# A ninth pair of gate/up tiles by seven products, with differences and low parts on GpSimd and a second norm that starts its x2 early

## The chip, the cores and the metric

The kernel runs on one NeuronCore of a Trainium2 chip. The core has a matrix engine (TensorE, PE), two engines for elementwise work with different strengths (VectorE, DVE; ScalarE, ACT), a general one (GpSimd, POOL) and a queue processor for transfers (SyncE, SP); PE writes to PSUM, all others work from SBUF or PSUM. The metric is the device time of one execution in microseconds. The median of several runs counts, and one more execution is recorded by the hardware profiler.

## The reference

One inference step of one layer, for a prompt of 1024 rows and a sample of 64 rows, all in fp32:

```python
def _layer(x, c, ...):
    mod = (silu(c) @ w_ada + b_ada)             # six shifts, scales and gates
    u = rmsnorm(x, g_pre_mix) * (1 + sc_m) + sh_m
    q, k, v, xr, yr, ga, gr = split(u @ w_in)
    attn_o = windowed_attention(q, k, v)        # 16 heads, 4 kv heads, window 128
    xc = causal_conv(xr);  h = rglru(xc)        # gated linear recurrence, 1280 wide
    rnn_o = h * gelu(yr)
    merged = sigmoid(ga) * (attn_o @ w_attn_o) + sigmoid(gr) * (rnn_o @ w_rnn_o)
    x = x + gt_m * rmsnorm(merged @ w_out, g_post_mix)
    u = rmsnorm(x, g_pre_ffn) * (1 + sc_f) + sh_f
    f = (silu(u @ w_ffn_gate) * (u @ w_ffn_up)) @ w_ffn_down
    return x + gt_f * rmsnorm(f, g_post_ffn)
```

The model width is 1024, the feed-forward width 2816, that is 22 tiles of 128 (`NF`). The new keys, values, convolution rows and states are returned too.

## The kernel before

Activations lie transposed, channels on the partitions and the 1088 rows (1024 + 64) along the free axis. A product in fp32 precision is made of three faster ones in the format fp32r: each operand is split into a high part (a copy rounded to fp32r) and a low part (what the rounding left), and `dense` adds high by high, high by low and low by high in PSUM. The high part of a weight (`wh`) is a copy on ACT, line 159, the low part (`wl`) a difference on DVE, line 163. `Stream` loads the weights over SP, keeps four raw tiles (`RAW`) and up to six split ones (`LIVE`) ahead.

The order of every engine's instructions is fixed when the kernel is built. `Sched` keeps a clock for each engine from estimated costs (`S.t`); PE's clock is `S.now`. Side work is written as generators in a heap: `dense` and the pair products give them a turn after each matmul (`S.poll`), and a generator that has yielded a time comes on when PE's clock has passed it. So the costs in `Sched`, not the chip, decide where in PE's row a transpose or a norm's product stands. The chip then runs each engine's row in this order and waits where an input isn't there.

The stages, by the trace: projections and norm from the start to about 72 us, then q and recurrent projections with attention beside them to 433 us, further projections and the recurrence to 759 us, the attention's and the recurrence's output projections to 977 us, the projection `w_out` with norms to 1084 us, gate and up tiles to 1573 us, the product with `w_ffn_down` to about 1848 us, and the last norm.

*Attention.* `attention()` (line 1097) goes through eight pairs of heads with nine `unit(j, t)` each (line 970), eight row tiles and the sample. A unit makes scores on PE (tag `sc`), then a softmax on DVE and ACT; after that four transposes (line 141, tag `pt`, from `s`) and a copy to `pts` on ACT. The products with V (tag `po`) of a unit are held back in `att["pv"]` and made by `run_pv` ahead of the next unit's transposes. Scores, transposes and these products lie between the matmuls of the projections (tag `d`). `attention()` waits at the end of each pair until all nine units are done.

*Norm chains.* `fin_chain(c)` (line 1429) follows the projection `w_out` for chunk c of 364, 364 and 360 columns. It makes a first norm from squares and products with ones (tag `ms` or `po`, `norm_stats`, line 544), takes the root (`rstd_of`), broadcasts by a product with `sel` (tag `pt`), forms x2 = x + gated norm in place of `mix`, m = 0 to 7, by two or three DVE instructions each, sends it to DRAM (`d_x2`) and takes the second norm's squares as each x2 tile is made; then come root and broadcast again and `make_u`, which writes u2 as high and low part (`u2h`, `u2l`). For the third chunk the squares of the second norm are added up on DVE into one tile first (`fold`, in `nb`), so that PE has one set of products with ones to do.

*Gate and up.* `NPLAIN` = 6 of the 22 tiles are made plainly by `f_tile` (line 1533), for each chunk 24 + 24 matmuls, then silu on ACT, the product on DVE (line 163, `hst<-hst,ps_d`), the high part on ACT, the low part on DVE (`hst<-hst`) and a store to `d_h` on POOL's queue. The order of tiles and chunks is `plain_jobs`: tiles 0 to 3 are spread so that the first two chunks are worked on while the third chunk's norm chain runs, tiles 4 and 5 come last. The other 16 tiles are made as eight pairs by `gu_pair` and `pair_product`: a 2 x 2 block product by seven instead of eight multiplications, with 168 matmuls of 272 columns for gate and as many for up. The right-hand factors are made once by `right_factors` (line 1557): per tile two sums `rec` of high and low part, four differences `tf` of 272 columns, their high part `rh` (ACT) and low part `rl` (DVE). All of this except `rh` is on DVE; the helper `calm` holds it until DVE's clock is less than 0.3 us ahead of PE's. The left-hand factors are sums of weight tiles `s1` to `s4` on DVE in `Stream.source`.

## Time and profile before

| | us |
|---|---|
| median of 3 runs (lowest, highest) | 1865.53 (1863.71, 1867.55) |
| the profiled execution's own time | 1862.13 |
| its span on the core | 1860.4 |
| PE busy | 1829.2 (98%), 12532 instructions |
| DVE busy | 1128.8 (61%), 2405 |
| ACT busy | 887.5 (48%), 1844 |
| POOL busy | 225.5 (12%), 371 |
| granted clock of TensorE, mean | 0.997 of full |

PE is busy when a matmul runs; its weight loads run beside it in a row of their own. The span is the time on the core from the first to the last recorded instruction, the own time of the execution is a little longer. A busy share is a mean over all stages, so stretches are read apart in the rows below. A group of instructions is named by line, engine, operation, output and inputs; behind the bar stand its busy time, the mean of one in ns, and the engine's idle time just ahead of them with what ended it.

### The profile page before, as it was taken

What the parts mean: (1) busy time and instruction counts of PE and PEld (TensorE: products, weight loads), DVE (VectorE), ACT (ScalarE), POOL (GpSimd) and SP (SyncE); (2) the same over time, 40 slices, a digit from 0 to 9 for tenths busy, and PEclk for the clock granted to TensorE, in tenths of its full rate; (3) what the DMA queues carried; (4) which work ended last, traced back from release to release, by engine and by line L of the source; (5) the groups of instructions that cost most, each with busy time, mean ns of one, the idle gap of its engine ahead of it and who ended that gap; (6) DMA issues with size and microseconds to landing.
All of it is one profiled execution on the core that took longest, in us unless ns stands there. A gap on an engine that the chain in (4) does not pass through costs nothing.

```text
span 1860.4 us, 32480 instructions
## 1 busy us (share of the span) xinstructions
PE 1829.2 (98%) x12532; PEld 1771.7 (95%) x12532; DVE 1128.8 (61%) x2405; ACT 887.5 (48%) x1844; POOL 225.5 (12%) x371
## 2 busy tenths in 40 slices
PE   7999999999999999999999999999999999999997
PEld 4999999999999999999999999999999999999997
DVE  6755556555877865264676878755556555245354
ACT  6655556654776665211225555433433344243444
POOL 0011111111111000201001111000000003212021
PEclk9999999999999999999999999999999999999998
DMA  8122212124344344955445554422222236959474
GB/s 330 58 67 76 83 60 71 66 97 151 117 150 174 112 151 152 396 166 210 141 152 180 181 177 153 141 71 99 98 94 94 96 109 233 349 175 337 125 227 126
DMA packets 116170, 281.15 MB, mean 151 GB/s; under 512 B 14800, under 2 KB 24272, under 8 KB 116016
## 3 DMA queue, kind: packets, MB, share of 16 engines
q1 hardware_dynamic: 81216, 155.71, 25.7%
q0 software_dynamic: 34800, 123.38, 18.4%
q8 instruction: 98, 1.61, 0.4%
q14 instruction: 56, 0.46, 0.1%
HBM read 210.46 MB, written 68.57 MB: 150 GB/s over the span
## 4 chain that ended last, share of the span: by engine, by line
PE 85%; issue 6%; DMA 4%; DVE 2%; ACT 2%; POOL 1%; SPq 0%; POOLq 0%; ACTq 0%; DVEq 0%
PE ps_d L132 67%; PE ps_sc L132 11%; PE ps_po L132 3%; PE ps_pt L141 2%; PE ps_pt L132 2%; DMA ho<-d_h 2%; DMA wr<-w 1%; DMA d_h<-hl 1%; ACT kh L159 1%; DMA xre<-d_x 1%; PE ps_ms L132 1%; ACT wh L159 1%; DMA x<-xT 0%; DVE wl L163 0%; POOL ho L186 0%
## 5 line engine op out<-in xcount | busy, mean ns | idle before, releaser
L163 DVE TENSOR_TENSOR wl<-wr,wh 128x512 fp32r<-128x512 f32 (+2 forms) x424 | 277.4, 674 | 232.4 <-ACT wh L159 231.5
L159 ACT ACTIVATE wh<-wr 128x512 fp32r<-128x512 f32 (+2 forms) x424 | 253.0, 610 | 269.3 <-PE ps_d L132 158.5
L132 PE MATMUL ps_d<-uh,wl 128*128 128x364 f32 (+1 forms) x1080 | 357.4, 331 | 0.0
L132 PE MATMUL ps_d<-uh,wh 128*128 128x364 f32 (+1 forms) x1080 | 356.4, 330 | 0.1
L132 PE MATMUL ps_d<-ul,wh 128*128 128x364 f32 (+1 forms) x1080 | 355.8, 329 | 0.6 <-DVE ul L167 0.6
L132 PE MATMUL ps_d<-ho,wh 128*128 128x416 f32 (+1 forms) x924 | 221.4, 327 | 3.6 <-ACT wh L159 2.5
L132 PEld LDWEIGHTS ps_d<-ul,wh 128*128 128x128 f32 x1080 | 203.1, 188 | 3.8 <-DVE ul L167 1.8
L132 PEld LDWEIGHTS ps_d<-uh,wl 128*128 128x128 f32 x1080 | 203.1, 188 | 2.3 <-issue 1.7
L132 PEld LDWEIGHTS ps_d<-uh,wh 128*128 128x128 f32 x1080 | 202.9, 188 | 1.7 <-ACT uh L159 1.4
L132 PEld LDWEIGHTS ps_d<-ho,wh 128*128 128x128 f32 x924 | 162.6, 190 | 6.1 <-ACT wh L159 2.9
L132 PE MATMUL ps_d<-ho,wl 128*128 128x416 f32 (+1 forms) x462 | 150.8, 326 | 0.7 <-DVE wl L163 0.7
L132 PE MATMUL ps_d<-u2h,wl 128*128 128x364 f32 (+2 forms) x480 | 150.6, 314 | 0.0
L132 PE MATMUL ps_d<-u2l,wh 128*128 128x364 f32 (+2 forms) x480 | 149.9, 312 | 0.0
L132 PE MATMUL ps_d<-u2h,wh 128*128 128x364 f32 (+2 forms) x480 | 149.8, 312 | 0.0
L159 ACT ACTIVATE wh<-ws 128x512 fp32r<-128x512 f32 x64 | 40.1, 627 | 112.5 <-DVE ws L163 112.5
L132 PEld LDWEIGHTS ps_d<-u2h,wl 128*128 128x128 f32 x480 | 90.2, 188 | 0.4
L132 PEld LDWEIGHTS ps_d<-u2h,wh 128*128 128x128 f32 x480 | 90.3, 188 | 0.0
L132 PEld LDWEIGHTS ps_d<-u2l,wh 128*128 128x128 f32 x480 | 90.3, 188 | 0.0
L132 PEld LDWEIGHTS ps_d<-ho,wl 128*128 128x128 f32 x462 | 87.7, 190 | 1.7 <-DVE wl L163 1.1
L167 DVE SCALAR_TENSOR_TENSOR adac<-ada,cs,adac 128x512 f32<-128x512 f32 x112 | 78.2, 745 | 14.4 <-DMA ada<-w_ada 14.4
L163 DVE TENSOR_TENSOR wl<-ws,wh 128x512 fp32r<-128x512 f32 x64 | 44.3, 692 | 67.9 <-ACT wh L159 67.1
L159 ACT ACTIVATE pts<-ps_pt 128x512 f32<-128x512 f32 (+2 forms) x80 | 40.0, 511 | 83.0 <-PE ps_pt L141 80.4
(350 smaller groups left out, 4325.5 us busy)
## 6 DMA issues: line engine op xcount, KB each, us to landing
wr<-w SPq DMA_DIRECT2D x268, 256.0 KB, 3.2
wr<-w_dn SPq DMA_DIRECT2D x120, 256.0 KB, 3.5
ho<-d_h POOLq DMA_DIRECT2D x44, 416.0 KB, 9.1
ada<-w_ada SPq DMA_DIRECT2D x48, 256.0 KB, 3.0
gl<-d_ga POOLq DMA_DIRECT2D x16, 544.0 KB, 6.7
d_h<-hh POOLq DMA_DIRECT2D x16, 544.0 KB, 4.2
d_h<-hl POOLq DMA_DIRECT2D x16, 544.0 KB, 5.4
ada<-w_ada SPq DMA_DIRECT2D x16, 512.0 KB, 9.7
```

Source lines behind the costliest of these rows:

```text
L132: self.nc.tensor.matmul(out, lhsT=w, rhs=x, start=start, stop=stop, skip_group_check=part)
L141: self.nc.tensor.transpose(out, in_, ident)
L159: self.nc.scalar.activation(out, in_, func, bias=bias, scale=scale, **kw)
L163: self.nc.vector.tensor_tensor(out, a, b, op=op)
L167: self.nc.vector.scalar_tensor_tensor(out, in0=a, scalar=s, in1=b, op0=op0, op1=op1)
```

## The change

1. `NPLAIN` goes from 6 to 4: tiles 4 and 5 leave the plain stage and become a ninth pair.
2. The factors' signs are chosen so that every difference is one subtraction: `s2` to `s4`, `t1` to `t4`, `partial`, `total`, and the last steps of gate and up no longer need a factor of -1.
3. A new helper `S.pool` issues an elementwise instruction on GpSimd. The four differences `tf` of each tile go there, and so does the low part of a plain tile's h, in a generator `finish` of its own; its store stays on POOL's queue behind it. `right_factors` makes up to two tiles at a time, each with its own `rec` and `tf`, and waits until six slots are free (five before); DVE's clock may be `CALM` = 1.5 us ahead.
4. `fin_chain` makes x2 in a generator `x2_make` that runs ahead of the squares by `AHEAD`; `norm_stats` issues the add of a folded square one step later.
5. A unit's transposes, with the held products with V ahead of them, become a generator `transposed` in a list `post`. The next unit takes them on right behind its scores, or the unit itself after 2.6 us. `attention()` goes to the next pair of heads when the nine units' scores are issued, and frees the pair's q then.

The core of the diff:

```diff
-NPLAIN = 6
+NPLAIN = 4
+CALM = 1.5
+AHEAD = 1.0
...
+    def pool(self, out, a, b, op, after=0.0):
+        self.nc.gpsimd.tensor_tensor(out, a, b, op=op)
+        return self._fin("pool", self._n(out) * 3.1e-3 + 0.05, after)
...
             if kind == "s2":
-                return s2, S.tt(s2, s1, a11, OP.add), 0
+                return s2, S.tt(s2, s1, a11, OP.subtract), 0
...
             f = S.act(sq, src, AF.Square, after=t)
+            if held:
+                add_up()
             if 0 < k < fold:
-                f = S.tt(ring[0][:, 0:n], ring[0][:, 0:n], sq, OP.add, after=f)
-                sq = ring[0][:, 0:n]
+                held.append((sq, f))
             if k >= fold - 1:
+                if held:
+                    sq, f = add_up()
                 pend.append((k, sq, f))
...
+        for g in post[:1]:
+            advance(g)
         t_sc = S.now + 0.1
...
+        g = [transposed(), S.now]
+        post.append(g)
+        limit = S.now + 2.6
+        while S.now < limit and g in post:
+            yield S.now + 0.1
+        while g in post:
+            advance(g)
+            yield max(g[1], S.now + 0.02)
...
-            dones = []
-            yield S.now + 1.0
             head_setup(j)
...
-            while not all(d[0] for d in dones):
-                yield S.now + 0.2
+            while att["sc"] < 9 * (j + 1):
+                yield S.now + 0.1
...
-        def x2_src():
+        done = []
+
+        def x2_make():
             for m in range(8):
...
-                yield mx(m), f
+                done.append((mx(m), f))
+                yield f - AHEAD
+
+        S.spawn(x2_make())
...
+    def finish(st, hi, lo, f2, dst, n):
+        yield f2 - 0.3
+        f3 = S.act(hi, lo, AF.Copy, after=f2)
+        yield f3 - 0.3
+        f4 = S.pool(lo, lo, f32(hi), OP.subtract, after=f3)
+        S.dma(QP, dst, f32(st[:, 0:2, 0:n]), after=f4)
+        st.free()
...
-            S.tt(t1, b11, b12, OP.subtract)
-            S.stt(t2, t1, -1.0, b22, OP.mult, OP.subtract)
-            S.tt(t3, b22, b12, OP.subtract)
-            f = S.stt(t4, t2, -1.0, b21, OP.mult, OP.subtract)
+            yield f - 0.3
+            for o, a, b in ((t1, b12, b11), (t2, b22, t1), (t3, b22, b12), (t4, b21, t2)):
+                f = S.pool(o, a, b, OP.subtract, after=f)
...
-                f = S.stt(g[p][:, 0, :], o, -1.0, g[p][:, 0, :], OP.mult, OP.mult, after=S.now + 0.1)
+                f = S.tt(g[p][:, 0, :], o, g[p][:, 0, :], OP.mult, after=S.now + 0.1)
```

The changed file's lines stand two to six further down: line 132 (matmul) becomes 134, 141 (transpose) 143, 163 (DVE's elementwise pair) 165, 167 becomes 173, 186 (transfers) 192, and line 169 is the new one on GpSimd.

What the new order looks like in three places. First PE's row in the attention stretch, around the scores of the 30th unit. Before (`ps_d` is a projection, `ps_po` a product with V, `ps_pt` a transpose, `ps_sc` the scores):

```order
L132 MATMUL ps_d_2757<-ul_331,wh_2180 128x360
L132 MATMUL ps_po_2732<-pts_1032,vs_85 64x128 x4
L141 MATMUL ps_pt_2761<-ident,s_1030 128x128 x4
L132 MATMUL ps_sc_2777<-kh_655,q_2175 128x256
L132 MATMUL ps_sc_2777<-kl_659,q_2175 128x256
L132 MATMUL ps_sc_2778<-kh_656,q_2176 128x256
L132 MATMUL ps_sc_2778<-kl_660,q_2176 128x256
```

The same place in the changed kernel:

```order
L134 MATMUL ps_d_2667<-uh_332,wl_2037 128x360
L134 MATMUL ps_sc_2677<-kh_655,q_2305 128x256
L134 MATMUL ps_sc_2677<-kl_659,q_2305 128x256
L134 MATMUL ps_sc_2678<-kh_656,q_2306 128x256
L134 MATMUL ps_sc_2678<-kl_660,q_2306 128x256
L134 MATMUL ps_po_2648<-pts_1032,vs_85 64x128 x4
L143 MATMUL ps_pt_2683<-ident,s_1030 128x128 x4
```

The products and transposes of earlier units moved from ahead of the scores to behind them. Second DVE's row at the third chunk's second norm, in the plain tiles, where `nb<-nb 128x360` adds up squares and line 174 (180) begins the root's arithmetic. Before:

```order
L163 TENSOR_TENSOR hst_11771<-hst_11771,ps_d_11773 128x364
L163 TENSOR_TENSOR hst_11771<-hst_11771 128x364
L163 TENSOR_TENSOR wl_11850<-wr_11686,wh_11849 128x512
L163 TENSOR_TENSOR nb_10867<-nb_10867 128x360
L163 TENSOR_TENSOR wl_11862<-wr_11696,wh_11861 128x512
L163 TENSOR_TENSOR hst_11844<-hst_11844,ps_d_11846 128x364
L163 TENSOR_TENSOR hst_11844<-hst_11844 128x364
L163 TENSOR_TENSOR wl_11896<-wr_11735,wh_11895 128x512
L174 TENSOR_SCALAR nb_10867<-ps_ms_11473 128x90
```

In the changed kernel:

```order
L165 TENSOR_TENSOR nb_10879<-nb_10879 128x360
L165 TENSOR_TENSOR rec_11458<-u2h_10789,u2l_10790 128x544
L165 TENSOR_TENSOR nb_10879<-nb_10879 128x360 x2
L165 TENSOR_TENSOR hst_11710<-hst_11710,ps_d_11712 128x364
L165 TENSOR_TENSOR wl_11764<-wr_11671,wh_11763 128x512
L165 TENSOR_TENSOR wl_11774<-wr_11681,wh_11773 128x512
L165 TENSOR_TENSOR rec_11458<-u2h_10797,u2l_10798 128x544
L180 TENSOR_SCALAR nb_10879<-ps_ms_11486 128x90
```

The low parts of h left DVE's row, the last adds stand together, the product of the gate tile comes directly behind them, and the sums of the factors stand between. Third POOL's row at the first plain tiles. Before, it holds only transfers:

```order
L186 DMA d_h<-hst_11404 128x2x364
L186 DMA xre_10868<-xT 128x360
L186 DMA d_x_75<-mix_10862 128x360
L186 DMA d_h<-hst_11499 128x2x364
L186 DMA xre_10868<-xT 128x360
L186 DMA d_x_75<-mix_10862 128x360 x2
```

In the changed kernel:

```order
L169 TENSOR_TENSOR hst_11390<-hst_11390 128x364
L192 DMA d_h<-hst_11390 128x2x364
L169 TENSOR_TENSOR tf_11447<-rec_11446 128x272
L169 TENSOR_TENSOR tf_11447<-rec_11446,tf_11447 128x272
L169 TENSOR_TENSOR tf_11447<-rec_11446 128x272
L169 TENSOR_TENSOR tf_11447<-rec_11446,tf_11447 128x272
L192 DMA xre_10880<-xT 128x360
L192 DMA d_x_75<-mix_10874 128x360 x2
```

The low part and four differences now stand ahead of the last load of `xre` and of the stores of x2.

## Rows read from the trace of the kernel before

**Rows 1.** The page, busy time, share of the span and instructions of each engine.

```profile
PE 1829.2 (98%) x12532; PEld 1771.7 (95%) x12532; DVE 1128.8 (61%) x2405; ACT 887.5 (48%) x1844; POOL 225.5 (12%) x371
```

**Rows 2.** Waits of PE: what it waited for, us in total, times, longest.

```profile
PE ps_ms L132 <- ACT sqs L159: 10.1, 6, 7.5
...
PE ps_d L132 <- DVE g L163: 1.1, 2, 1.0
```

**Rows 3.** Busy us (instructions) by stretch: PE, weight loads, DVE, ACT, POOL; clock, DMA.

```profile
100.00:433.00 333.00, 333.00 (x2450) 304.53 (x2448) 194.92 (x784) 195.91 (x655) 47.80 (x89) 1.00 0.22 74
1084.58:1232.39 147.81, 147.81 (x930) 146.76 (x930) 115.82 (x231) 70.61 (x130) 17.74 (x27) 1.00 0.40 136
1184.60:1232.39 47.79, 47.79 (x290) 47.79 (x290) 32.46 (x57) 15.38 (x25) 4.35 (x6) 1.00 0.22 80
1232.39:1572.77 340.38, 339.21 (x2689) 337.77 (x2689) 193.98 (x350) 133.11 (x257) 29.08 (x41) 1.00 0.33 110
```

**Rows 4.** Timeline of PE in the attention stretch: start us, us, engine, line, operation.

```profile
202.52 0.33 PE L132 MATMUL ps_d<-uh,wl 128*128 128x360 f32 x1
202.69 0.32 PE L132 MATMUL ps_d<-ul,wh 128*128 128x360 f32 x1
202.94 0.66 PE L132 MATMUL ps_po<-pts,vs 128*64 128x128 f32 x8
```

**Rows 5.** Groups of DVE in the plain tiles, 1084.58 to 1232.39 us.

```profile
L163 DVE TENSOR_TENSOR wl<-wr,wh 128x512 fp32r<-128x512 f32 x46 | 30.4, 688 | 7.0 <-ACT wh L159 6.9
...
L167 DVE SCALAR_TENSOR_TENSOR u2l<-mix,mod,u2h 128x364 fp32r<-128x364 f32 (+2 forms) x24 | 10.5, 466 | 0.0
L167 DVE SCALAR_TENSOR_TENSOR mix<-mix,gsf,ps_pt 128x364 f32<-128x364 f32 (+2 forms) x24 | 10.4, 461 | 1.1 <-PE ps_pt L132 1.1
...
L163 DVE TENSOR_TENSOR hst<-hst 128x364 f32<-128x364 f32 (+1 forms) x17 | 9.1, 537 | 10.7 <-ACT hst L159 10.7
L163 DVE TENSOR_TENSOR hst<-hst,ps_d 128x364 f32<-128x364 f32 (+1 forms) x17 | 8.9, 526 | 1.4 <-issue 0.9 <-PE ps_d L132 0.3
L167 DVE SCALAR_TENSOR_TENSOR tf<-tf,rec 128x272 f32<-128x272 f32 x16 | 7.0, 438 | 0.3
L163 DVE TENSOR_TENSOR tf<-rec 128x272 f32<-128x272 f32 x16 | 6.9, 434 | 0.0
```

**Rows 6.** Groups of POOL in the tail, 1780 to 1861 us, shapes kept apart.

```profile
L1756 POOL TENSOR_TENSOR fo<-fo,aux 128x416 f32<-128x416 f32 x3 | 4.1, 1380 | 14.5 <-ACT aux L159 14.5
L1757 POOL TENSOR_TENSOR xre<-xre,fo 128x416 f32<-128x416 f32 x3 | 3.8, 1267 | 0.2
```

**Rows 7.** Busy time by stretch, as rows 3, with and without GpSimd work.

```profile
1783.07:1791.60 8.53, 8.53 (x75) 8.53 (x74) 8.43 (x10) 4.23 (x9) 8.24 (x7) 1.00 0.38 106
1791.60:1795.64 4.04, 4.04 (x37) 4.04 (x36) 3.97 (x8) 0.98 (x2) 1.11 (x2) 1.00 0.86 263
```

**Rows 8.** Groups of DVE there: two beside GpSimd's work, two right behind it.

```profile
L163 DVE TENSOR_TENSOR wl<-wr,wh 128x512 fp32r<-128x512 f32 (+1 forms) x3 | 4.4, 1482 | 0.0
...
L163 DVE TENSOR_TENSOR fo<-fo,ps_sc 128x416 f32<-128x416 f32 x3 | 1.7, 579 | 0.6 <-ACT aux L159 0.6
...
L163 DVE TENSOR_TENSOR wl<-wr,wh 128x512 fp32r<-128x512 f32 x3 | 2.0, 679 | 0.0
...
L163 DVE TENSOR_TENSOR fo<-fo,ps_sc 128x416 f32<-128x416 f32 x2 | 1.1, 575 | 0.0
```

**Rows 9.** Timeline of PE behind the third chunk's second squares, to the broadcast.

```profile
1136.17 0.43 PE L132 MATMUL ps_d<-u2h,wl 128*128 128x364 f32 x1
...
1141.26 0.35 PE L132 MATMUL ps_pt<-nb,sel 128*128 128x90 f32 x2
```

**Rows 10.** Timeline of ACT there; in brackets the idle time before and its end.

```profile
1136.44 0.51 ACT L159 ACTIVATE hst<-hst 128x364 fp32r<-128x364 f32 x1 [1.33 <-DVE hst L163]
...
1137.49 1.28 ACT L159 ACT_TABLE_LOAD   x1
```

**Rows 11.** Timeline of DVE there, the last step of y.

```profile
1140.64 0.25 DVE L167 SCALAR_TENSOR_TENSOR nb<-nb 128x90 f32<-128x90 f32 x1
```

More of the change, by code (lines that the diff above doesn't have):

```diff
@@ L554, in products, with add_up @@
                      stop=k == 7, fp32=True, conc=4)
+        held = []
+        def add_up():
+            sq, f = held.pop()
+            total = ring[0][:, 0:n]
+            return total, S.tt(total, total, sq, OP.add, after=f)
         k = 0
@@ L968, in run_pv, with advance @@
             yield from pv[1]()
+    post = []
+    def advance(g):
+        if g[1] > S.now:
+            return
+        try:
+            g[1] = next(g[0])
+        except StopIteration:
+            post.remove(g)
     def unit(j, t):
@@ L1112, in attention @@
             att["done"] = j
+        while not all(d[0] for d in dones):
+            yield S.now + 0.2
         S.slack = 0.8
@@ L1478, in x2_src @@
                     S.rel(tag2, f)
-                yield mx(m), f
+                done.append((mx(m), f))
+                yield f - AHEAD
+        S.spawn(x2_make())
+        def x2_src():
+            for m in range(8):
+                while len(done) <= m:
+                    yield None
+                yield done[m]
         yield from norm_stats(st, n, [nb[:, i, :] for i in range(3)], x2_src(), FOLD[c][1])
@@ L1559, in right_factors, with tile_factors @@
         b0 = PAIRS[p]
-        rec = A.get("rec", F32, [2, 2 * HALF])
-        tf = A.get("tf", F32, [4, HALF])
-        def calm():
-            while S.t["dve"] > S.now + 0.3:
-                yield max(S.now + 0.1, S.t["dve"] - 0.2)
-        for i in range(4):
-            while len(A.free) < 5:
+        def tile_factors(i):
+            while len(A.free) < 6:
                 yield S.now + 0.5
+            rec, tf = A.get("rec", F32, [2, 2 * HALF]), A.get("tf", F32, [4, HALF])
             hi, lo = A.get("rh", F32R, [4, HALF]), A.get("rl", F32R, [4, HALF])
-            yield from calm()
@@ L1572, in right_factors @@
             for j, k in enumerate((i, i + 4)):
[L1573 removed]
+                while S.t["dve"] > S.now + CALM:
+                    yield max(S.now + 0.1, S.t["dve"] - CALM + 0.1)
+                f = S.tt(rec[:, j, :], f32(u2[k][0][:, b0:b0 + 2 * HALF]), f32(u2[k][1][:, b0:b0 + 2 * HALF]), OP.add)
             b11, b12, b21, b22 = (rec[:, j, h * HALF:(h + 1) * HALF] for j in range(2) for h in range(2))
@@ L1581, in right_factors @@
+            rec.free()
             f = S.act(hi[:, :, :], tf[:, :, :], AF.Copy, after=f)
-            yield f
-            yield from calm()
+            yield f - 0.3
+            while S.t["dve"] > S.now + CALM:
+                yield max(S.now + 0.1, S.t["dve"] - CALM + 0.1)
             S.tt(lo[:, :, :], tf[:, :, :], f32(hi[:, :, :]), OP.subtract, after=f)
+            tf.free()
             right[p][i] = (hi, lo)
-        rec.free()
-        tf.free()
+        jobs = []
+        for i in range(4):
+            while len(jobs) - sum(d[0] for d in jobs) >= 2:
+                yield S.now + 0.3
+            jobs.append(S.spawn(tile_factors(i)))
+            yield S.now + 0.2
@@ L1589, in all_factors @@
+        while not all(d[0] for d in jobs):
+            yield S.now + 0.2
     def all_factors():
@@ L1633, in partial @@
             j = (2, 1, 3)[step]
-            S.act(v[:, j, :], o, AF.Copy, after=t, scale=-1.0 if step == 1 else 1.0)
+            S.act(v[:, j, :], o, AF.Copy, after=t)
         def total(v, step, o):
-            j, op = ((2, OP.add), (1, OP.subtract), (3, OP.add))[step - 3]
-            return j, S.tt(v[:, j, :], v[:, j, :], o, op, after=S.now + 0.1)
+            j = (2, 1, 3)[step - 3]
+            return j, S.tt(v[:, j, :], v[:, j, :], o, OP.add, after=S.now + 0.1)
         def gate(p, step, o):
@@ L1649, in gate @@
             else:
-                S.act(g[p][:, 0, :], o, AF.Silu, after=S.now + 0.1, scale=-1.0)
+                S.act(g[p][:, 0, :], o, AF.Silu, after=S.now + 0.1)
         def up(p, step, o):
```

65 lines of the change are left out of this document (33 added, 32 removed).

## The prediction

> **What bounds the kernel now.** I read the page's busy times first. TensorE (PE) is busy 98% of the span and the next engine, VectorE (DVE), 61% [rows 1], so a change is worth what it does to the length of PE's own row of work, unless it makes PE wait. Then the waits of PE: in the stretch that the change touches most, gate and up tiles at 1084.58 to 1572.77, the only wait is the one for g, 1.1 us in two pieces [rows 2]; the longest of the whole span, 10.1 us for sqs, lies at the program's start. Last the busy times by stretch [rows 3]. In the plain tiles PE is busy for all of 147.81 us, in the pair products for 339.21 of 340.38 us, in the attention stretch for all of 333.00 us. So no wait is there to be won in any of them: what can be won is the number of columns that PE has to stream, and what can be lost is its cover. The cover that matters is DVE in the plain tiles, 115.82 of 147.81 us, with ScalarE (ACT) and GpSimd (POOL) far from full.
>
> **Part 1, tiles 4 and 5 as a ninth pair.** The two tiles are the last plain work of before, alone in 1184.60 to 1232.39: 2 tiles x 2 weights x 72 = 288 matmuls, 47.79 us with PE busy throughout (the row counts 290 with the ones cut at its ends) [rows 3]. What comes for them is one more pair of 2 x 168 = 336 matmuls of 272 columns. Eight such pairs take 340.38 us with their 1.17 us of idle time [rows 3], so one takes 340.38 / 8 = 42.55 us. More matmuls, but shorter ones: 47.79 - 42.55 = **5.24 us less**. This is priced from whole stages, so weight loads, drains and the small waits for g are in it. The sign changes cost and gain nothing on PE; DVE forms with a scalar that become plain ones take the same (434 against 438 ns for a difference) [rows 5].
>
> **Part 2, the differences and low parts on GpSimd.** 32 differences of 272 columns and 12 low parts (eight of 364, four of 360) go there. GpSimd did such operations at 416 columns in 1380 and 1267 ns [rows 6], 1.32 us for 416, so I estimate 0.865 us for 272 and 1.155 us for a low part: 32 x 0.865 + 12 x 1.155 = 41.5 us, on an engine that was busy for 17.74 us in this stage [rows 3], mostly with issuing. DVE is spared 7.0 + 6.9 us of differences and 9.1 us of low parts [rows 5]; 5 fewer products with the gate take off 2.6 us, eight fewer weight splits 5.5 us, and the second chunk's u2, made before the plain tiles begin in the new order, some 8 x (461 + 466) ns = 7.4 us [rows 5]. That leaves 115.8 - 13.9 - 9.1 - 2.6 - 5.5 - 7.4 = 77.3 us in a stage of 147.81 - 47.79 = 100.0 us: 77%, as dense as before (78%).
>
> But the two engines hinder each other. Late in the program GpSimd works 8.24 us of a stretch of 8.53 us, and there ten DVE instructions take 8.43 us; right behind it, eight of the same kinds take 3.97 us [rows 7]. Per instruction 0.843 against 0.496 us: ten lose 3.5 us to 8.24 us of GpSimd, 0.42 us for each. A weight split takes 1482 instead of 679 ns, while the product with an operand in PSUM stays at 579 against 575 [rows 8]. With this price 41.5 us cost DVE 17.4 us: 94.7 of 100.0 us. It fits, but the slack is gone, and everything that PE waits for from DVE comes somewhat later.
>
> The row shows a loss of 0.42, not of 1. The Trainium skill (SBUF — State Buffer, section on SBUF's two separate sides) says that DVE and GpSimd take a common port pair as an exclusive lock, for a whole instruction, when the DVE one reads two operands from SBUF; by that rule the loss would be 1 and the stage would not fit. What a loss of 1 would give stands with the first rival.
>
> POOL's queue also carries transfers. Behind the first four differences stands the last load of the residual xre for the third chunk's x2. The four take 3.5 us, and DVE has some 25 instructions (over 12 us at 0.5 us) between the sums they wait for and the add that needs the load. So I cost it at nothing; without that cover it is 3.5 us on DVE. The stores of h wait for the low parts, and no one reads them before the down stage.
>
> **Part 3, x2 ahead of its squares.** The planner takes the third chunk's second norm earlier in PE's row: its broadcast now stands 345 matmuls before the first pair (57 us at 0.166) instead of 545 (90 us). The chain behind the square products took from 1136.17 to 1140.89, 4.7 us, when the last step of y ended [rows 9, 11]; PE had 30 matmuls (5.0 us) to put between, and began the broadcast at 1141.26 without a wait [rows 9]. In the new order 24 stand there, 4.0 us. So 0.7 us are missing. On ACT a root stands behind the copy of a gate tile that waits for DVE, 1.33 us at that place before, and behind its own 1.28 us table load [rows 10]; the new order puts the product that feeds the copy directly behind the last fold adds on DVE, so some more is lost. I take **1.0 us** of PE wait. Bounds: 0, if DVE arrives ahead; 8 us, if DVE is half a dozen instructions of 1.48 us late.
>
> **Part 4, attention.** The transposes and products with V move behind the next unit's scores. PE leaves its fp32r work for the fp32 block as often as before (72 and 8 times): the first matmul of a block comes 0.25 us after the one ahead, against 0.17 us between two of the others [rows 4], and this step is paid as often in both orders. PE didn't wait in 333.00 us [rows 3]. The units end some 30 us earlier in PE's row (181 dense matmuls at 0.165), which packs the same DVE and ACT work (195 and 196 of 333 us [rows 3]) from 59% to about 65%. The smallest distance from scores to their transposes grows from 4.4 to 6.8 us of PE work, so cover grows too. I cost it at **0**, with bounds -0.5 and +1 us (half a dozen such steps of 0.08 us fewer, a dozen more). What ends earlier only frees space.
>
> **Sum.** -5.24 + 0 + 0 + 1.0 = -4.24 us. The profiled execution took 1862.13 us; the sum makes 1857.9 of it. It lies 3.40 us under the median of the three runs (1865.53), so against the median: 1865.53 - 4.24 = **1861.3 us**. About 0.2%, 3.7 us, is what a measurement of this kernel can tell from no change; the forecast lies just over that.
>
> **Rivals.**
> (a) *DVE falls behind in the plain tiles and the gain is eaten.* For it: 94.7 of 100.0 us leave 5 us of slack over a stage in which work doesn't come evenly. Against it: weights are split up to six parts ahead, which is 72 matmuls or 12 us, and before no PE wait showed with DVE at 78%. At a loss of 1 for each GpSimd microsecond DVE would need 77.3 + 41.5 = 118.8 us, 18.8 too much; less the 12 us of splits ahead PE waits 6.8 us, and with the norm's 1.0 us the change ends at 1865.53 - 5.24 + 7.8 = 1868.1. Between there and the forecast lie waits of 2 to 8 us at the norm or for splits: 1862.3 to 1868.1.
> (b) *Slower: GpSimd is late with the factors for the first pair.* From the third chunk's u2, 12 us of PE work behind the broadcast, 45 us are left to the first pair. In them GpSimd makes some 20 differences and 6 low parts: 20 x 0.865 + 6 x 1.155 = 24.2 us at the rows' pace. The rows were taken with DVE half free of the conflict; if GpSimd itself is held up by DVE, its operations stretch. It decides from 45 / 24.2 = 1.9 times the rows' pace; at 2.5 times it takes 60.5 us, PE waits 15.5 us less the 4 us in which the first product can use those that are there: 11 us. 1865.53 - 5.24 + 11 = 1871.3, slower than before.
> (c) *More gain.* The norm costs nothing, and the waits for g go: 1.17 us in eight pairs, 1.3 us in nine. 1865.53 - 5.24 - 1.3 = 1859.0.
> That the change doesn't do what it says is no case: the written order shows 48 more matmuls, and the moved rows.
>
> **How the numbers follow.** The forecast (waits of 0 to 2 us, 1860.3 to 1862.3) has 0.48, rival (a) 0.31, (b) 0.11, (c) 0.10. Over 0.2% faster means under 1861.8: all of (c) and 0.42 of the forecast, 0.52. Within 0.2%: the rest of the forecast and nearly all of (a), 0.36. Slower: (b), and the tail of (a), 0.12. The range goes from a little under (c), 1858.5, to the end of (a), 1868.1, so that (b) and tails are left out.
>
> **What would show it.** Right: a pair stage of about 9 x 42.5 = 383 us, a plain stage of 100 to 101 us with a PE wait of about 1 us at the broadcast of the third chunk's second norm, weight splits beside GpSimd at 0.9 to 1.5 us, an attention stretch without PE waits. Wrong: PE waits for weight splits in the plain tiles (a), or for rl or rh at the first pair (b); a GpSimd difference that takes well over 0.9 us; PE idle in the attention stretch; or a pair that takes other than 42.5 us.

## The result and the profile after

The changed kernel takes 1873.29 us (median of five runs, 1871.66 to 1876.08), the kernel before 1863.71 us beside it (1863.25 to 1867.55): a ratio of 1.0052, with a 95% interval of 1.0041 to 1.0062. It is slower by some 9.6 us where 4.2 us less were forecast, and outside the range. The profiled execution of the change took 1871.66 us, its span is 1869.6 us, 9.2 us longer than before.

By the first matmul of each stage, the spans compare so (us):

| stage | before | after | difference |
|---|---|---|---|
| start to the attention's output projection | 759.5 | 761.3 | +1.8 |
| that projection | 96.7 | 98.9 | +2.2 |
| the recurrence's output projection | 120.7 | 120.8 | +0.1 |
| `w_out` with norms | 107.7 | 108.3 | +0.6 |
| gate and up: plain tiles and pairs | 488.2 | 495.5 | +7.3 |
| down product to the end | 287.6 | 284.9 | -2.7 |

The gate and up stage should have become 5.2 us shorter; it became 7.3 us longer, so 12.5 us are to be found there. The down product's 2.7 us have another source: before, PE waited 1.76 us in the middle of it and ran 3.41 us at half clock from 1810.1 on; after, no such wait and no such stretch stands there. The page of the changed kernel, busy time of each engine, answers [rows 1]:

```profile
PE 1829.0 (98%) x12580; PEld 1770.6 (95%) x12580; DVE 1143.0 (61%) x2385; ACT 897.9 (48%) x1859; POOL 273.9 (15%) x413
```

PE has 48 matmuls more and the same busy time, where 5 us less were expected: some matmuls ran slower. DVE has 20 instructions fewer and is busy 14.2 us longer. PE's waits between 1088 and 1585 us, the stretch in which before had 1.1 us [rows 2]:

```profile
PE ps_d L134 <- ACT g L161: 4.1, 1, 4.1
PE ps_ms L134 <- DVE nb L165: 2.2, 1, 2.2
PE ps_d L134 <- DVE g L165: 1.8, 3, 0.9
PE ps_d L134 <- DVE wl L165: 1.3, 2, 1.0
PE ps_sc L134 <- DVE rl L165: 0.4, 1, 0.4
```

The norm's square products wait 2.2 us for the folded sum, weight splits cost 1.3 us, the first pair 0.4 us for `rl` and 4.1 us for a copy of `g` on ACT: 8.0 us beside the waits for g on DVE that were there before. Busy times by stretch, plain tiles, pairs and two short pieces of them (columns as in [rows 3]; behind the POOL entry stands the granted clock):

```profile
1089.20:1194.24 105.04, 101.53 (x634) 99.38 (x633) 94.38 (x150) 56.66 (x102) 58.81 (x62) 0.98 0.47 147
1194.24:1584.70 390.46, 384.10 (x3026) 381.94 (x3025) 223.60 (x400) 153.41 (x295) 34.90 (x48) 0.99 0.32 108
...
1128.39:1131.80 3.41, 3.41 (x19) 3.27 (x12) 3.41 (x6) 3.22 (x4) 2.35 (x3) 0.50 0.53 181
...
1203.48:1210.31 6.83, 4.51 (x20) 4.51 (x21) 2.92 (x5) 3.60 (x9) 1.78 (x2) 0.50 0.61 202
```

The plain stage is 105.04 us long, with DVE busy for 94.38. In two stretches the granted clock is 0.50 (1.2 GHz); one begins 0.2 us behind the 2.2 us wait, the other within the 4.1 us wait. That is the rest of the 12.5 us, as the first pair shows on PE (start, us; idle time before it in brackets):

```profile
1205.80 0.59 PE L134 MATMUL ps_d<-rh,wh 128*128 128x272 f32 x1 [4.14 <-ACT g L161]
1206.19 0.43 PE L134 MATMUL ps_d<-rh,wl 128*128 128x272 f32 x1
1206.42 0.43 PE L134 MATMUL ps_d<-rl,wh 128*128 128x272 f32 x1
1206.65 0.43 PE L134 MATMUL ps_d<-rh,wh 128*128 128x272 f32 x1
```

Matmuls of 272 columns follow each other at 0.23 us instead of 0.126: 20 of them lose 2.1 us, and 11 of 364 columns in the first stretch lose 1.5 us. Waits of 8.0 us and 3.6 us of slow matmuls are 11.6 of the 12.5 us; the waits for `g` on DVE grew by 0.7.

The copy of `g` itself is quick. What it stood behind shows ACT's timeline there:

```profile
1202.37 0.63 ACT L161 ACTIVATE wh<-ws 128x512 fp32r<-128x512 f32 x1 [3.16 <-DVE ws L165]
1204.44 0.63 ACT L161 ACTIVATE wh<-ws 128x512 fp32r<-128x512 f32 x1 [1.44 <-DVE ws L165]
1204.98 0.49 ACT L161 ACTIVATE hst<-hst 128x360 fp32r<-128x360 f32 x1
1205.37 0.38 ACT L161 ACTIVATE g<-ps_d 128x272 f32<-128x272 f32 x1
```

ACT waited 3.16 and 1.44 us for DVE's weight sums, with the copy queued behind. Before, ACT waited for sums at this place too (1.28 and 1.44 us), but the copy came 5.2 us behind the pair's first matmul (1232.39) and PE didn't wait; now it comes 11.1 us behind it (1194.24). Before:

```profile
1234.94 0.63 ACT L159 ACTIVATE wh<-ws 128x512 fp32r<-128x512 f32 x1 [1.28 <-DVE ws L163]
1237.01 0.63 ACT L159 ACTIVATE wh<-ws 128x512 fp32r<-128x512 f32 x1 [1.44 <-DVE ws L163]
1237.55 0.39 ACT L159 ACTIVATE g<-ps_d 128x272 f32<-128x272 f32 x1
```

DVE begins the sums late because it is still at older work: in the 30.30 us up to the end of the first weight sum it is busy for 29.75, and in the 8.3 us ahead of the norm's products for 8.13.

```profile
1120.00:1128.30 8.30, 6.13 (x42) 5.86 (x43) 8.13 (x18) 4.46 (x9) 3.40 (x5) 1.00 0.84 264
1164.87:1195.17 30.30, 29.25 (x178) 28.73 (x178) 29.75 (x28) 11.26 (x19) 25.68 (x22) 1.00 0.43 138
```

So DVE is late, and ACT hands its lateness on to PE. The groups of DVE and GpSimd from 1089.2 us to the first pair's early steps (before: [rows 5, 6]):

```profile
L165 DVE TENSOR_TENSOR wl<-wr,wh 128x512 fp32r<-128x512 f32 x39 | 35.1, 926 | 8.1 <-ACT wh L161 8.1
L165 DVE TENSOR_TENSOR rec<-u2h,u2l 128x544 f32<-128x544 f32 x16 | 16.0, 1026 | 0.0
L165 DVE TENSOR_TENSOR rl<-tf,rh 128x1088 fp32r<-128x1088 f32 x8 | 11.9, 1491 | 0.2 <-ACT rh L161 0.2
...
L165 DVE TENSOR_TENSOR hst<-hst,ps_d 128x364 f32<-128x364 f32 (+1 forms) x12 | 6.3, 522 | 0.9 <-PE ps_d L134 0.9
```

```profile
L169 POOL TENSOR_TENSOR tf<-rec,tf 128x272 f32<-128x272 f32 x16 | 17.9, 1116 | 1.3 <-DVE rec L165 0.7
L169 POOL TENSOR_TENSOR tf<-rec 128x272 f32<-128x272 f32 x16 | 16.6, 1040 | 2.3 <-DVE rec L165 1.5 <-PE ps_pt L134 0.7
L169 POOL TENSOR_TENSOR hst<-hst 128x364 f32<-128x364 f32 x8 | 9.5, 1185 | 18.0 <-ACT hst L161 17.9
...
L169 POOL TENSOR_TENSOR hst<-hst 128x360 f32<-128x360 f32 x4 | 5.0, 1259 | 9.6 <-ACT hst L161 9.6
```

GpSimd's 44 instructions take 49.0 us where 41.5 were forecast. On DVE splits take 926 ns instead of 688, sums of the factors 1026 and low parts of the factors 1491, both shown free of GpSimd's work in the first experiment below; the product with its operand in PSUM is unchanged (522 against 526).

### The profile page after: what moved, and what is told of

Same layout as the page of the kernel before. It is cut to its first block, busy times and chain, and to the rows that moved or that the text cites. A ratio compares the mean times of both kernels' runs of the same rounds, so it can differ in the third digit from the quotient of the medians.

```text
span 1869.6 us, 32581 instructions
## 1 busy us (share of the span) xinstructions
PE 1829.0 (98%) x12580; PEld 1770.6 (95%) x12580; DVE 1143.0 (61%) x2385; ACT 897.9 (48%) x1859; POOL 273.9 (15%) x413
## 4 chain that ended last, share of the span: by engine, by line
PE 62%; issue 22%; DMA 6%; DVE 6%; ACT 2%; POOL 2%; SPq 0%; POOLq 0%; DVEq 0%; ACTq 0%
PE ps_d L134 51%; PE ps_sc L134 5%; PE ps_po L134 3%; PE ps_pt L143 2%; DVE wl L165 2%; DMA ho<-d_h 2%; DMA aol<-d_ao 1%; POOL d_h L192 1%; PE ps_pt L134 1%; DMA d_h<-hl 1%; ACT wh L161 1%; DVE rec L165 1%; DMA ada<-w_ada 1%; DVE mix L173 1%; ACT kh L161 1%
## 5 line engine op out<-in xcount | busy, mean ns | idle before, releaser
L165 DVE TENSOR_TENSOR wl<-wr,wh 128x512 fp32r<-128x512 f32 (+2 forms) x422 | 286.8, 697 | 236.8 <-ACT wh L161 235.7
L134 PE MATMUL ps_d<-u2h,wl 128*128 128x272 f32 (+2 forms) x408 | 126.5, 310 | 1.3 <-DVE wl L165 1.3
L134 PE MATMUL ps_d<-u2h,wh 128*128 128x272 f32 (+2 forms) x408 | 126.1, 309 | 0.0
L134 PE MATMUL ps_d<-u2l,wh 128*128 128x272 f32 (+2 forms) x408 | 125.8, 308 | 0.0
L161 ACT ACTIVATE wh<-ws 128x512 fp32r<-128x512 f32 x72 | 45.2, 627 | 133.2 <-DVE ws L165 133.2
L165 DVE TENSOR_TENSOR wl<-ws,wh 128x512 fp32r<-128x512 f32 x72 | 49.9, 692 | 74.7 <-ACT wh L161 74.7
L134 PE MATMUL ps_d<-rh,wh 128*128 128x272 f32 x288 | 84.3, 293 | 6.0 <-ACT g L161 4.1
L134 PE MATMUL ps_sc<-rl,wh 128*128 128x272 f32 x288 | 83.2, 289 | 0.4 <-DVE rl L165 0.4
L134 PE MATMUL ps_d<-rh,wl 128*128 128x272 f32 x288 | 83.5, 290 | 0.0
L134 PE MATMUL ps_sc<-rh,wh 128*128 128x272 f32 x288 | 83.5, 290 | 0.0
```

The lines of the kernel that those rows point to most:

```text
L134: self.nc.tensor.matmul(out, lhsT=w, rhs=x, start=start, stop=stop, skip_group_check=part)
L161: self.nc.scalar.activation(out, in_, func, bias=bias, scale=scale, **kw)
L165: self.nc.vector.tensor_tensor(out, a, b, op=op)
```

## The experiments

The theory after this reading: GpSimd's work hinders VectorE, VectorE comes late to the norm and to the first pair, and the slow clock adds to it. Rivals: the shorter plain stage alone (less cover), another part of the change, or an order that is too early even for a free VectorE.

**e9, GpSimd's work taken out of the same order.**

```diff
-        self.nc.gpsimd.tensor_tensor(out, a, b, op=op)
+        k = 16
+        self.nc.gpsimd.tensor_tensor(a[:, 0:k], a[:, 0:k], b[:, 0:k], op=op)
...
-            f = S.act(hi[:, :, :], tf[:, :, :], AF.Copy, after=f)
+            f = S.act(hi[:, :, :], rec4, AF.Copy, after=f)
```

> The changed kernel with the same order on TensorE, VectorE and ScalarE, but GpSimd's 44 operations work on 16 columns only (the differences are left out and the factors' parts are made from the sums; the low parts of h are left out but for 16 columns). So the waits on GpSimd and its place in the order stay and its work, and with it the hindrance of VectorE (17 us), goes. Theory: that hindrance makes VectorE late for the norm and the first pair; without it the waits of 2.2, 1.0 and 4.1 us and the half-clock stretches behind them (5 us together of loss) go, and the weight splits in the plain tiles take 0.69 instead of 0.93 us: 1861 to 1863 us. Rival: the order itself is too early even for an unhindered VectorE, and the time stays at 1870 to 1874 us.

The low parts `rl` are made from the sums as well (that part of the edit isn't shown). Measured: 1860.72 us, ratio 0.9983 (0.9973 to 0.9992). The one wait of PE in the gate and up stage:

```profile
PE ps_d L134 <- DVE g L165: 2.2, 3, 1.3
```

The groups of DVE in its plain part:

```profile
L165 DVE TENSOR_TENSOR wl<-wr,wh 128x512 fp32r<-128x512 f32 x39 | 25.9, 690 | 12.3 <-ACT wh L161 12.3
L165 DVE TENSOR_TENSOR rec<-u2h,u2l 128x544 f32<-128x544 f32 x16 | 11.1, 720 | 0.0
L165 DVE TENSOR_TENSOR rl<-rec,rh 128x1088 fp32r<-128x1088 f32 x8 | 10.2, 1289 | 0.3 <-ACT rh L161 0.3
```

The two stretches, plain tiles and pairs:

```profile
1091.10:1190.16 99.06, 99.06 (x635) 97.96 (x633) 79.37 (x155) 59.97 (x108) 28.77 (x64) 1.00 0.49 160
1190.16:1573.20 383.04, 380.61 (x3026) 379.08 (x3025) 219.41 (x395) 149.78 (x289) 32.36 (x46) 1.00 0.32 109
```

All 8.0 us of waits and both slow stretches are gone, and the stage is 482.1 us: 6.1 less than before, somewhat more than the ninth pair promised. So the order was not too early for a free VectorE, and GpSimd's 44 operations are the cause of the loss. e9 also shortens the way through GpSimd itself (sum, difference, copy), so it can't tell by itself a hindered VectorE from a late GpSimd. The trace of the change can: PE's two long waits ended on VectorE's results, behind the two stretches above in which VectorE hardly paused. The hindrance in the three groups is 39 x 0.236 + 16 x 0.306 + 8 x 0.202 = 15.7 us.

**e3, the same work on VectorE, and e2, the ninth pair alone.** e3 replaces the call on GpSimd by `self.tt(out, a, b, op, after)`; e2 is the kernel before with

```diff
-NPLAIN = 6
+NPLAIN = 4
```

> The changed kernel with the differences and low parts issued on VectorE at the same places. If VectorE being slowed beside GpSimd is the cause (17 us of VectorE time), the waits shrink to 0 to 2 us: 1859 to 1862 us. If the stage is simply too short, VectorE takes 13.9 + 6.4 = 20.3 us of work back and loses 17 us of hindrance, a wash, and the time stays at 1870 to 1876 us.

Measured: 1875.29 us, 1.0056 (1.0041 to 1.0071). The expectation for too short a stage held: the waits only move, to 5.3 us for `rh`, 2.4 for `rl` and 1.0 for `hst`. Moving 20 us to GpSimd and leaving it on VectorE cost the same time, but not in the same way: in e3's plain stage VectorE is busy for only 86.5 of 100.3 us, and the last four sums of factors start at 1196.30 us, 7 us behind the pair's first matmul. So the order holds them back, and not only a full engine.

> The kernel before with NPLAIN = 4 alone: the ninth pair, with differences and low parts still on VectorE, old attention order, old norm. If the missing cover is the cause, VectorE has 77.3 + 13.9 + 6.4 = 97.6 us of work for 100 us and TensorE waits at the first pair, 1868 to 1876 us. If GpSimd's part is the cause, this kernel shows the pair's gain without it: 1858 to 1860 us.

Measured: 1891.31 us, 1.0140 (1.0124 to 1.0155), worse than expected. PE waits 16.7 us for `rh` and 6.2 for `rl`, and the clock is at half for 30.7 us behind 1193.4. e3 also has all of this work on VectorE and is 16 us faster, with the factors of two tiles under way at a time, looser pacing, the early x2 and the attention order. Some of these parts of the change do help, then; which of them isn't separated.

**e1 and e8, six plain tiles again.** e1 is the changed kernel with `NPLAIN = 6`. e8 undoes the early x2 and the attention order as well, so that next to GpSimd's work only signs and pacing are new.

> The changed kernel with NPLAIN = 6 again, so eight pairs and six plain tiles; GpSimd's differences and low parts, the early x2 and the attention order stay. If the loss comes from the plain stage having 48 us less of TensorE work to cover VectorE's work, the waits of the third chunk's second norm and of the first pair go and the kernel comes out near the kernel before, 1862 to 1865 us against its 1863.7. If another part of the change (attention order, early x2) costs the 4 us that the profile of the changed kernel shows outside the gate and up stage, it stays slower, 1867 to 1869 us.

Measured: 1870.95 us, 1.0037 (1.0025 to 1.0049): slower than before with the old amount of cover, and above both expectations. PE waits 2.1 us at the norm's products, 1.4 us at its broadcast and 1.3 us for splits. The loss at the norm doesn't come from the ninth pair, then.

> Six plain tiles and eight pairs, old attention order, old x2 and squares; only the signs, the two tiles' factors at a time and GpSimd's differences and low parts are new. Theory: with 48 us more cover and the square products late enough, GpSimd's hindrance of VectorE costs TensorE nothing: 1862 to 1865 us, and the 6.7 us that e1 lost belong to the early x2 and the attention order. Rival: the hindrance alone makes TensorE wait, 1867 us or more.

Measured: 1878.32 us, 1.0079 (1.0064 to 1.0094); the rival held. PE's waits in the gate and up stage:

```profile
PE ps_ms L134 <- DVE nb L165: 8.2, 1, 8.2
PE ps_d L134 <- DVE wl L165: 1.7, 2, 1.5
```

With the differences gone from VectorE's clock (and the looser pacing) the planner sets the norm's products 30 matmuls (5.0 us) earlier than before, behind 259 instead of 289 of the plain stage, and VectorE comes later than it did: the products start 55 us into the stage, before 51. GpSimd's work without the early x2 costs more than the whole change, although two more plain tiles cover it.

**e6 and e5, the early x2 and the attention order undone.**

> The changed kernel with x2 made in step with its squares again and the folded adds not held back. The square products then stand 52 matmuls (8.6 us) later in TensorE's order. Theory: the planner had put them too early for a VectorE that GpSimd slows, so the 2.2 us wait of the norm and the 3.4 us at half clock behind it go; the first pair's waits stay or grow a little, since the third chunk's u2 comes later: 1870 to 1873 us. Rival: without the early x2 the factors come so late that the first pair waits over 8 us: 1877 us or more.

Measured: 1878.44 us, 1.0081 (1.0064 to 1.0098). The theory of this run fell: the wait at the norm grows from 2.2 to 8.2 us. The rival's time came, but not its way, as the first pair waits 2.9 us and not over 8. The early x2 with the later adds is worth 5 us; why VectorE comes so much later without them isn't shown.

> The changed kernel with the attention part undone (transposes ahead of the next scores, a wait at the end of each pair of heads). Theory: the new attention order lets other work take the buffers first, so that the last loads of the attention's output are issued some 6 us later and TensorE waits 1.1 to 2.1 us for them at the output projection, as in all four runs with the new order; undone, that wait goes and the time falls by about 2 us, to 1871 us beside 1873. Rival: the wait is chance or is made good elsewhere, and the time stays at 1873.

Measured: 1873.80 us, 1.0054 (1.0039 to 1.0069). The wait for the attention's output is gone (the projection takes 96.7 us again), but the time isn't lower: in this run the `w_out` stage took 109.4 instead of 108.3 us. The attention order makes no difference clear of noise; the wait of 1.1 to 2.1 us that it brings shows in every run with it, and why undoing it saves nothing is not settled.

**e4, the planner told of the hindrance.**

```diff
+        self.t["dve"] = max(self.t["dve"], after) + 0.42 * (self._n(out) * 3.1e-3 + 0.05)
```

> The changed kernel, but the planner charges VectorE's clock 0.42 us for each microsecond of GpSimd's work, so that norms and squares stand later in TensorE's order. If a wrong order is the cause, the 2.2 us wait of the norm and most of the 4.1 us wait in the first pair go, and with them the stretches at half the granted clock: 1860 to 1864 us. If VectorE's work does not fit whatever the order, the norm's wait goes but the first pair's stays or grows: 1868 to 1873 us.

Measured: 1881.90 us, 1.0087 (1.0069 to 1.0105), worse than both expectations. The norm's wait stays at 2.3 us and the first pair waits 9.8 us for `rh` and 3.1 for `rl`: the factors are held until VectorE's clock is less than 1.5 us ahead, so a clock that runs ahead would hold them too long; no run tests this reading.

**e7, e10 and e11, more room for VectorE.** All three have the old attention order and eight jobs for the plain tiles instead of ten, so that two tiles' weights are split once less each. e10 and e11 hold the first half's factors back until the norm is through (all but one tile, and all), with its products 4 us later.

```diff
-    plain_jobs = [(0, (0,)), (1, (0,)), (0, (1,)), (1, (1,)), (2, (0, 1)), (3, (0, 1)), (0, (2,)), (1, (2,)), (2, (2,)),
-                  (3, (2,))] + [(f, (0, 1, 2)) for f in range(4, NPLAIN)]
+    plain_jobs = [(0, (0,)), (1, (0, 1)), (0, (1,)), (2, (0, 1)), (3, (0, 1, 2)), (0, (2,)), (1, (2,)), (2, (2,))]
```

> The kernel of e5 with another order of the four plain tiles: tile 1 for chunks 0 and 1 in one go, tile 3 for all three, so that two tiles' weights are loaded and split once less each: eight jobs for ten, eight weight splits fewer on VectorE (8 x 0.69 to 0.93 = 5.5 to 7.4 us) and as many on ScalarE. Theory: VectorE's lateness at the first pair is the cause, about 6 to 8 us; then the 4.1 us wait there shrinks to 0 to 1 us and the half-clock stretch with it: 1862 to 1866 us. Rival: GpSimd's differences are what is late there, and the relief of VectorE changes little: 1869 to 1871 us.

Measured: 1867.71 us, 1.0024 (1.0015 to 1.0034), a little over the theory's range. The wait at the first pair is gone, the one at the norm has grown to 5.7 us: relief of VectorE does help the first pair, and the lateness shows at the other place.

> e7 with two changes of order: of the first half's factors only one tile is made before the third chunk's second norm is through, and that norm's products come 4 us later than the planner would have them (they stand behind 200 plain matmuls, as against 195 in e7). VectorE is relieved of some 5 us of sums, low parts and hindrance ahead of the norm. Theory: e7 lost only at the norm (5.7 us and 6.8 us at half clock), where VectorE was late; the wait shrinks to 0 to 1 us and e7's 1867.7 falls by 6 to 8 us, to 1860 to 1862 us, under the kernel before. Rival: what is put off comes back as waits for the first pair's factors, 1866 us or more.

Measured: 1866.23 us, 1.0011 (1.0002 to 1.0020). No wait is left at the norm's products, 1.2 us at its broadcast, and 3.5 us are back at the first pair.

> As e10, but no factors at all are made before the norm is through; its products then stand behind 175 plain matmuls. VectorE is relieved of some 10 us ahead of the norm, which stands 3.3 us earlier. Theory: no wait at the norm, all eight tiles' factors in the 62 us behind it, VectorE needs about all of them: waits of 0 to 3 us at the first pair, 1860 to 1864 us. Rival: GpSimd and VectorE cannot do them in that time, 5 us or more of waits there: 1867 us or more.

Measured: 1871.47 us, 1.0041 (1.0029 to 1.0053): 4.5 us for `g` and 2.1 us for a split. In none of these three orders does VectorE's lateness go; it shows at the norm or at the pair.

**e12 and e13, a kernel that does all the work without GpSimd.** e12 is e7 with the differences and low parts on VectorE (`S.tt` for `S.pool` in both calls). e13 loads more raw weight tiles ahead:

```diff
-        RAW, LIVE = 4, 6
+        RAW, LIVE = 6, 5
```

> e7 with GpSimd's 32 differences and 12 low parts issued on VectorE, where the planner counts them; old attention order, eight jobs for the plain tiles, early x2, ninth pair. Theory: GpSimd took 20.3 us of work off VectorE and gave 17 us back as hindrance that the planner's clock doesn't know, so the norm was put too early. On VectorE the work costs about as much, but it is counted, and the eight weight splits fewer (5.5 us) give the room that the kernel without GpSimd's work in the tenth experiment's order didn't have: no PE wait over 1 us in the plain tiles and the first pair, a plain stage of 100 us, nine pairs of 42.6 us, and 1864.0 - 5.2 = 1858 to 1861 us. Rival: VectorE's sum is too large with or without GpSimd (77.3 + 20.3 - 5.5 = 92.1 of 100 us, and the work is uneven): waits of 4 us or more remain, 1864 us or more.

Measured: 1866.56 us, 1.0016 (1.0007 to 1.0025). The time is the rival's, the waits aren't: the norm no longer waits, and the first pair waits 2.8 us. Beside e7 (1.0024) the work on VectorE instead of GpSimd makes no difference clear of noise. But VectorE wasn't short of time ahead of the pair, as its timeline shows:

```profile
1181.76 0.69 DVE L165 TENSOR_TENSOR wl<-wr,wh 128x512 fp32r<-128x512 f32 x1
1187.33 0.69 DVE L165 TENSOR_TENSOR ws<-wr,wr 128x512 f32<-128x512 f32 x1 [4.87 <-DMA wr<-w]
```

It stood still for 4.87 us, for raw weights whose loads went out from 1177.88 to 1181.33 us, each 0.03 us behind the end of a split that freed a raw tile of the plain tiles.

> e12 with six raw weight tiles loaded ahead instead of four, and five split ones instead of six (the memory allows no more). In e12 VectorE stood still for 4.87 us ahead of the first pair's first weight sum, whose four raw tiles were loaded only when the last plain tile's were split, and TensorE then waited 2.8 us and ran 6.8 us at half clock. Theory: with GpSimd's work gone, this late load is all that is left in the first pair; with two more raw tiles the weights are there, the wait goes, and the time falls by 4 to 6 us to 1860 to 1862 us, under the kernel before (1863.4 to 1864.3). Rival: VectorE itself is short of time in the squeezed stage, the wait moves to the plain tiles or stays, and the time stays at 1865 to 1868 us.

Measured: 1856.92 us, 0.9960 (0.9946 to 0.9974): 7.6 us faster than the kernel before, and 16 us faster than the change. The two stretches, plain tiles and pairs:

```profile
1087.40:1191.43 104.03, 101.35 (x633) 99.46 (x633) 91.74 (x191) 57.22 (x101) 13.37 (x21) 0.98 0.41 135
1191.43:1571.10 379.67, 379.67 (x3026) 379.67 (x3025) 220.15 (x395) 152.03 (x288) 31.98 (x45) 1.00 0.33 109
```

PE's waits in both:

```profile
PE ps_d L134 <- ACT wh L161: 1.7, 1, 1.7
PE ps_d L134 <- DVE wl L165: 1.0, 1, 1.0
```

The pairs run without any wait; both waits and a half-clock stretch of 3.4 us lie in the plain stage, in which VectorE is busy for 91.74 of 104.03 us. The gate and up stage is 483.7 us, 4.5 less than before: most of the ninth pair's gain, in a kernel that does all the work.

**e14 and e15, the same two numbers in the kernels before and after.**

> The kernel before with six raw weight tiles and five split ones, nothing else. If e13's 7.5 us come mainly from the ninth pair (5.2 us), this kernel gains only what the waits for g in the pair stage (1.1 us) and a slow stretch of the down stage are worth: 1861 to 1863.5 us. Rival: the earlier loads alone make e13's gain, 1857 to 1859 us, and the ninth pair adds nothing.

Measured: 1861.69 us, 0.9984 (0.9975 to 0.9993), as the first theory said. In the kernel before the earlier loads are worth 2.9 us, and 1861.69 - 1856.92 = 4.8 us are left for what else e13 has: the ninth pair, its order of jobs, the pacing and the early x2. In e12 the same loads were worth 9.6 us (1866.56 - 1856.92).

> The changed kernel with six raw and five split tiles, GpSimd's work as in the change. Theory: GpSimd's hindrance makes VectorE late for the norm and the first pair, and earlier loads do not change that: it loses most of the 8 us of waits still, 1868 to 1873 us. Rival: the late loads were the cause of the changed kernel's waits too: 1858 to 1862 us.

Measured: 1870.17 us, 1.0033 (1.0021 to 1.0045). Earlier loads take about 3 us off the change too (the two intervals overlap a little), but it stays slower than before, with these waits in the stage:

```profile
PE ps_d L134 <- DVE wl L165: 2.7, 3, 1.8
PE ps_ms L134 <- DVE nb L165: 2.1, 1, 2.1
PE ps_d L134 <- ACT wh L161: 1.9, 1, 1.9
```

One kernel wasn't run: e7, which has GpSimd's work and eight jobs, with six raw tiles. e15 has the raw tiles with the change's ten jobs, e13 the raw tiles with eight jobs and no work on GpSimd. Whether e13's gain needs the work taken off GpSimd, or only fewer splits and earlier loads together, stays open.

## Why the prediction was wrong

**Part 1 was right.** Nine pairs take 379.67 us in e13, 42.2 us for each, and 383.04 us in e9, 42.3 without its waits for `g`, against 42.55. The gate and up stage of these two kernels, whose PE has its cover, is 4.5 and 6.1 us shorter than before, around the 5.24 us forecast.

**Part 2 had the right price and the wrong verdict.** The forecast put the hindrance at 17.4 us; the three groups show 15.7. It put VectorE at 94.7 us; it was busy for 94.38. That the sum came so near is partly luck: without the hindrance e9 shows 79.4 us where 77.3 were put (of `u2l` four instructions fall ahead of the stage, not eight), and GpSimd worked 49.0 us, not 41.5. The step that failed is the next one, "It fits, but the slack is gone", and with it the first rival's lower weight. 94.7 of 100.0 us was read as work that can lie anywhere in the stage. It can't: VectorE also stands still for 8.1 us in all, waiting for high parts on ACT, and two places in PE's row have a date, the norm's products and the first pair. In e9 VectorE needs 79.4 us and PE waits for nothing but `g` on DVE; in the change 94.4, and PE waits 8.0 us more than that. The first rival's hard end, 6.8 + 1.0 = 7.8 us of waits, was met by chance: its sum has VectorE at 118.8 us and the 6.8 us spread over the splits, while the trace has 2.2 us at the norm, 4.5 at the first pair and 1.3 for splits.

**Part 2's first sum hid the exchange.** I booked 23 us off VectorE and 17.4 us onto it in two separate steps, and compared the balance with the stage's length. Set side by side, 32 differences at 0.436 and 12 low parts at 0.537 are 20.4 us, and 15.7 of them come back: GpSimd's 49.0 us bought under 5 us. On the clock the two places cost the same (e3: 1875.29 against 1873.29 us, with intervals that overlap).

**Part 3 was mis-sized.** The missing 1.0 us at the norm was priced from the chain behind its products. At the broadcast, where the prediction looked for it, PE didn't wait. The wait came at the products themselves, 2.2 us for the last folded add, because the planner put them where a VectorE without hindrance would be: 207 matmuls into the stage, against 289 before. An order made by costs that leave the hindrance out is itself a term; without the early x2 (e6, e8) that wait is 8.2 us. Charging the planner 0.42 us for each microsecond of GpSimd's work (e4) didn't take it away.

**A term was missing:** 3.6 us of matmuls at half clock behind the two longer waits. With the rival's 7.8 us and this, 1865.53 - 5.24 + 7.8 + 3.6 = 1871.7 us would have been the sum, slower than before; beside it stand 0.7 us more of waits for `g` and 2.0 us outside the gate and up stage, by the table.

**Part 4 held** in the attention stretch: from the first projection's matmul to the attention's output projection both kernels take 733.3 us (26.2 to 759.5 before, 28.0 to 761.3 after). The sentence "What ends earlier only frees space" was wrong: the attention's last outputs were loaded 6 us later, at 759.7 instead of 753.6 us, and PE waited 1.8 us for them. e5 shows that undoing it doesn't change the total beyond noise.

**Rival (b)** gave the sign but not the way. GpSimd was not late with the factors: its differences took 1.04 to 1.12 us, 1.25 times the rows' pace and under the 1.9 from which it would decide; PE waited 0.4 us for `rl`. The side that lost was VectorE.

## What to carry to other kernels

In this kernel work moved from VectorE to GpSimd wasn't removed from VectorE, where both read their operands from SBUF: 20.4 us went and 15.7 came back. So set what is taken off beside what comes back as longer instructions. Telling the planner's clock of it is not enough by itself; e4 did so and was slower still.

A busy share doesn't tell whether a stage fits. In the change PE waited 8.0 us with VectorE busy for 94.4 of the plain stage's 105.0 us, in e12 2.8 us at the first pair with 88.5 of 100.1, and in e13 2.7 us in the plain tiles and nothing in the pairs, with 91.7 of 104.0. Look for the results with a date, for what VectorE itself waits for, and for the waits that it hands on through another engine's queue.

A saving on the bound engine (here 5 us) comes out only when the cover that it removes (48 us of matmuls) is made good. e13 did it without GpSimd, by less splitting of the same weights and earlier loads.

## What the runs showed of the hardware

The hindrance isn't a sharing of speed, as the mean of 0.42 might suggest: in these rows one engine waits until the other's instruction is through. On VectorE and then GpSimd, in the changed kernel around 1149 and 1165 us:

```profile
1148.72 0.69 DVE L165 TENSOR_TENSOR wl<-wr,wh 128x512 fp32r<-128x512 f32 x1 [1.47 <-ACT wh L161]
1149.63 1.15 DVE L165 TENSOR_TENSOR wl<-wr,wh 128x512 fp32r<-128x512 f32 x1 [0.22 <-ACT wh L161]
...
1164.87 1.04 DVE L165 TENSOR_TENSOR wl<-wr,wh 128x512 fp32r<-128x512 f32 x1 [1.55 <-ACT wh L161]
```

```profile
1149.16 1.08 POOL L169 TENSOR_TENSOR hst<-hst 128x364 f32<-128x364 f32 x1 [10.06 <-ACT hst L161]
...
1164.39 0.98 POOL L169 TENSOR_TENSOR hst<-hst 128x364 f32<-128x364 f32 x1 [1.62 <-ACT hst L161]
```

The split that starts at 1149.63 ends at 1150.78, 0.54 us behind the end of GpSimd's instruction (1150.24); the one at 1164.87 ends at 1165.91, again 0.54 us behind GpSimd's end (1165.37), though a free split takes 0.69 us from its start. It is no chance of two places: of the plain stage's 39 splits 17 take longer than 0.70 us, and 16 of these end 0.54 to 0.56 us behind the end of a GpSimd instruction. The split at 1148.72 was there first and took its 0.69 us. Then GpSimd is the one that waits: its low part of 1149.16 ends 0.83 us behind that split and takes 1.08 us, against 0.98 us for the one at 1164.39, which came first.

The prediction cited the Trainium skill (SBUF — State Buffer, section on SBUF's two separate sides) for an exclusive lock between the two engines for an instruction with two operands in SBUF, and set the row's 0.42 against it. The trace agrees with the Trainium skill that the lock is whole. A loss of 1 for each GpSimd microsecond, as the prediction read it, doesn't follow from that. GpSimd's instruction waits as well when it comes second, so its measured time holds waiting (a difference takes 0.77 us at the least, 1.04 to 1.12 on average), and VectorE's instructions with an operand in PSUM (522 ns in the change) run meanwhile. How much each of the two takes off the loss isn't separated. On GpSimd's side no instruction in these traces has an operand in PSUM, so the opening's words on engines that work from SBUF or PSUM are not shown for it.

The granted clock went to 0.50 (1.2 GHz) for 3.4 us behind a wait of 2.2 us and for 6.8 us at one of 4.1 us; in e7 for 6.8 us at a wait of 5.7 us, in e2 for 30.7 us where waits of some 3 us follow each other. Not every wait brings it, and not for the same time: e1 waited 2.1 us at the same place, and no such stretch stands in its gate and up stage; e5, with waits of 2.2 and 4.1 us as in the change, has none behind the first and 3.4 us at the second.
